# The second SwiGLU's gate and up by seven block products, its down product in three passes

## The chip, the core and the metric

The kernel runs on one core of one Trainium2 chip. The metric is the time of one execution on the device in microseconds (us), the median of several runs. TensorE (PE in the profile) multiplies matrices out of SBUF into PSUM; VectorE (DVE), ScalarE (ACT) and GpSimd (POOL) work on tiles of 128 partitions; SyncE (SP) issues nearly all the loads and stores, in the order of its program.

## What is computed

One layer of a hybrid encoder on 1024 tokens (S) of width 1024 (D): a SwiGLU half-step, a mixer (differential attention beside a bidirectional Mamba-2 scan, one input and one output projection), a second SwiGLU half-step, and a last norm. The width inside a SwiGLU is 2816, which is 22 blocks of 128.

```
def swiglu(x, w_gate, w_up, w_down):
    return (jax.nn.silu(x @ w_gate) * (x @ w_up)) @ w_down

f = swiglu(rmsnorm(h, ffn1_pre_g), ffn1_w_gate, ffn1_w_up, ffn1_w_down)
h = h + 0.5 * rmsnorm(f, ffn1_post_g)
m = hybrid_mixer(rmsnorm(h, mix_pre_g), layer_idx, p)
h = h + rmsnorm(m, mix_post_g)
f = swiglu(rmsnorm(h, ffn2_pre_g), ffn2_w_gate, ffn2_w_up, ffn2_w_down)
h = h + 0.5 * rmsnorm(f, ffn2_post_g)
return rmsnorm(h, final_g)
```

## The kernel before, in words

Every matrix product is done in float32 precision by three matmuls (`mm3`, lines 180 to 182): each operand is split into a high part (a cast on ACT, L174) and a low part (a subtraction, mostly on DVE, L175), and hi·hi, hi·lo and lo·hi are added in PSUM.

The first SwiGLU, up to 717 us, has two halves. `blocks_gate_up` (L304) takes tokens, D and FF in two halves each and needs seven block products for a matrix instead of eight: sums of blocks of the activations stand ready as seven transposed operands b11, b21, b22, t1 to t4 (`blocks_prep`, L259), sums of blocks of the weights are made on the fly on POOL (L363 to L366), and the partial results are joined on DVE. A matrix of 2 FF blocks takes 84 matmuls of 512 columns, a pair of gate and up 168; there are 11 pairs. The product g goes to DRAM (`gd`, L329). `blocks_down` (L418) then goes three times through the 22 FF blocks, for 3, 3 and 2 token tiles, and each pass reads its part of g and all of w_down again; 1056 matmuls in all. What runs around its start is set by pools: the loads of its first weights go into the same ring of three raw buffers that gate and up used.

The mixer follows. Its output projection (`out_rounds`, its additions at L1297 and L1299) runs as filler beside the attention and keeps its sums of all 8 token tiles in SBUF (acc0 to acc7). The last rounds of it are finished at the start of the second SwiGLU.

The second SwiGLU (`ffn`, L462) is direct: for each of 11 chunks of two FF blocks 192 matmuls of gate and up for the 8 token tiles, and 96 of down, whose results are added to acc in SBUF on DVE (L500). g never leaves SBUF. The first and the last chunk work in pieces of 256 columns: `pre2` finishes the output projection tile by tile, adds the residual (`residual`, L237 and L238), norms and transposes (`norm_T`, L208) while the first chunk runs; the last chunk lets each token tile go on to its norms as it is done. Two weight tiles of the first chunk are loaded and split in the end of the attention (`ahead`).

`rstd` (L198 to L200) sums squares on ACT and takes the power on POOL. L165 and L175 are those of one helper for many tiles, so groups are told apart by the tile's name.

In the changed kernel the lines of these functions stand 47 or more lines further down: L165 becomes L212, L175 L222, L208's norm is done at L318, L281 to L284 are L333 to L336, L329 is L381, L434 is L486.

## Time and profile before

| | |
|---|---|
| median of 3 runs | 2638.22 us (2634.17 to 2638.88) |
| the profiled execution | 2636.09 us |
| span in its profile, first to last instruction | 2634.3 us |
| mean granted clock of TensorE | 0.986 |
| first SwiGLU: gate and up / down | about 400 / 250.6 us |
| second SwiGLU, from 1832 us to the end | 802 us |

The profile is of one execution. An engine's busy time counts its instructions; matmuls are pipelined, so that two of them overlap in the listing, and their number in a stretch with its length gives the pitch. In a timeline the bracket behind an instruction is the idle time of its engine before it and what released it. The granted clock is given as a share of full speed.

### The profile page before, as it was taken

Reading aid. Unit: us, or ns where it says so; the run is one execution under the profiler, and the core shown is the slowest. Engines: PE = TensorE matmul, PEld = TensorE weight load, DVE = VectorE, ACT = ScalarE, POOL = GpSimd, SP = SyncE. Lnnn points to the kernel's source line nnn. Section 1 sums busy time; section 2 is a strip of 40 time slices with the busy share of each in tenths; the row PEclk is TensorE's granted clock in tenths of the full one; section 3 lists DMA queues with packets and bytes.
Section 4 is the critical chain, followed back from the end, with each engine's and each line's share of the span. In section 5 each row is a group of like instructions: output and inputs, shape, how many; then the busy total and the mean of one; then the engine's idle time right before and its main releaser. Section 6 shows DMA issues by size and latency. Waiting matters only on the chain.

```text
span 2634.3 us, 32959 instructions
## 1 busy us (share of the span) xinstructions
PE 2524.5 (96%) x12504; PEld 2121.9 (81%) x12504; DVE 1518.2 (58%) x2125; ACT 1003.1 (38%) x1709; POOL 818.9 (31%) x748
## 2 busy tenths in 40 slices
PE   6999999999999999999979999999999999999996
PEld 4888888888888898877758888888888888888885
DVE  7655554464736553777737888888723333333336
ACT  5333222343535543454436555555431111111113
POOL 7332321020210474344326666666300000000005
PEclk8999999999999999999989999999999999999998
DMA  4222222755722675555464444451521111111112
GB/s 152 88 80 74 95 82 78 243 200 174 254 93 94 177 245 199 166 185 182 133 176 106 117 113 123 103 146 53 173 66 35 48 48 48 49 48 48 48 41 104
DMA packets 133406, 309.07 MB, mean 117 GB/s; under 512 B 13696, under 2 KB 62720, under 8 KB 128384
## 3 DMA queue, kind: packets, MB, share of 16 engines
q1 hardware_dynamic: 114912, 245.37, 28.1%
q0 software_dynamic: 10016, 57.42, 8.1%
q10 hardware_dynamic: 8320, 4.19, 0.5%
q8 instruction: 98, 1.61, 0.3%
q14 instruction: 60, 0.49, 0.1%
HBM read 227.50 MB, written 79.43 MB: 117 GB/s over the span
## 4 chain that ended last, share of the span: by engine, by line
PE 83%; DVE 6%; ACT 3%; POOL 3%; issue 2%; DMA 2%; SPq 0%; DVEq 0%; POOLq 0%; ACTq 0%
PE po L182 7%; PE po L180 7%; PE po L181 7%; PE b L180 5%; PE b L181 5%; PE b L182 5%; PE pp L180 5%; PE pp L181 5%; PE pp L182 5%; PE pg L180 3%; PE pg L181 3%; PE pg L182 3%; PE pu L181 3%; PE pu L180 3%; PE pu L182 3%
## 5 line engine op out<-in xcount | busy, mean ns | idle before, releaser
L199 POOL TENSOR_SCALAR rstd<-rstd 128x1 f32<-128x1 f32 x64 | 29.1, 454 | 982.1 <-ACT junk L198 981.1
L175 DVE TENSOR_TENSOR split<-raw,split 128x1024 fp32r<-128x1024 f32 (+3 forms) x220 | 249.9, 1142 | 128.1 <-ACT split L174 127.2
L174 ACT CAST split<-raw 128x1024 fp32r<-128x1024 f32 (+3 forms) x227 | 192.8, 860 | 237.4 <-issue 86.9
L500 DVE TENSOR_TENSOR acc<-acc,po 128x512 f32<-128x512 f32 x160 | 108.6, 686 | 210.4 <-PE po L182 210.3
L1044 ACT ACTIVATE e<-sc,st 128x1024 f32<-128x1024 f32 x128 | 143.3, 1120 | 165.1 <-DVE st L1040 165.1
L180 PE MATMUL pp<-hT,split 128*128 128x512 f32 x384 | 153.4, 399 | 10.5 <-DVE o L909 10.5
L1040 DVE TENSOR_REDUCE st<-sc 128x1 f32<-128x1024 f32 x128 | 150.5, 1217 | 12.6 <-PE sc L1038 12.6
L181 PE MATMUL pp<-hT,split 128*128 128x512 f32 x384 | 151.9, 396 | 0.0
L182 PE MATMUL pp<-hT,split 128*128 128x512 f32 x384 | 151.9, 396 | 0.0
L180 PE MATMUL po<-odd,g 128*128 128x512 f32 x352 | 138.6, 396 | 7.0 <-DVE acc L500 7.0
L181 PE MATMUL po<-odd,g 128*128 128x512 f32 x352 | 138.2, 392 | 0.0
L182 PE MATMUL po<-odd,g 128*128 128x512 f32 x352 | 138.1, 394 | 0.0
L181 PE MATMUL b<-hT,split 128*128 128x512 f32 x352 | 137.8, 391 | 0.3 <-DVE attc L1008 0.3
L182 PE MATMUL b<-hT,split 128*128 128x512 f32 x352 | 137.6, 391 | 0.0
L180 PE MATMUL b<-hT,split 128*128 128x512 f32 x352 | 137.5, 392 | 0.1
L1051 POOL TENSOR_SCALAR e<-e,st 128x768 f32<-128x768 f32 x64 | 75.7, 1182 | 181.7 <-DVE st L1050 138.2
L182 PE MATMUL po<-split,gs 128*128 128x512 f32 x334 | 131.9, 395 | 0.0
L181 PE MATMUL po<-split,gs 128*128 128x512 f32 x334 | 131.9, 395 | 0.0
L180 PE MATMUL po<-split,gs 128*128 128x512 f32 x334 | 131.3, 395 | 0.0
L1053 POOL TENSOR_TENSOR e<-e,e 128x768 f32<-128x768 f32 x64 | 118.3, 1848 | 5.4
L174 ACT CAST g<-sg 128x512 fp32r<-128x512 f32 (+1 forms) x52 | 28.7, 552 | 238.5 <-DVE acc L500 107.8
L180 PE MATMUL pp<-split,hT 128*128 128x512 f32 (+1 forms) x320 | 117.4, 367 | 0.0
(376 smaller groups left out, 7240.7 us busy)
## 6 DMA issues: line engine op xcount, KB each, us to landing
raw<-in_w_down_dram SPq DMA_DIRECT2D x88, 512.0 KB
raw<-in_w_gate_dram SPq DMA_DIRECT2D x45, 512.0 KB
raw<-in_w_up_dram SPq DMA_DIRECT2D x45, 512.0 KB
qkd<-o SPq DMA_DIRECT2D x64, 256.0 KB
qk<-qkd POOLq DMA_DIRECT2D x16, 1024.0 KB, 7.9
gd<-w SPq DMA_DIRECT2D x43, 256.0 KB
vd<-o SPq DMA_DIRECT2D x32, 256.0 KB
kb<-qkd POOLq DMA_DIRECT2D x16, 512.0 KB, 5.2
```

The lines of the kernel that those rows point to most:

```text
L174: self.nc.scalar.copy(out=hi, in_=src)
L175: (eng or self.nc.vector).tensor_tensor(out=lo, in0=src, in1=hi.bitcast(F32), op=ALU.subtract)
L180: mm(out=out, lhsT=a[0], rhs=b[0], start=start, stop=False, **kw)
L181: mm(out=out, lhsT=a[0], rhs=b[1], start=False, stop=False, **kw)
L182: mm(out=out, lhsT=a[1], rhs=b[0], start=False, stop=stop, **kw)
L199: nc.gpsimd.tensor_scalar(out=r[:, 1:2], in0=r[:, 0:1], scalar1=k / n, scalar2=k * EPS, op0=ALU.mult, op1=ALU.add)
L500: nc.vector.tensor_tensor(out=a[:, ns], in0=a[:, ns], in1=po[n], op=ALU.add)
L1040: nc.vector.tensor_reduce(out=X["st"][:, j:j + 1], in_=pc, op=ALU.max, axis=AX.X, negate=True)
L1044: self.nc.scalar.activation(out=X["e", j], in_=X["sc", j], func=AF.Exp, bias=st[:, j:j + 1], accum_out=st[:, 2 + j:3 + j])
L1051: G.tensor_scalar(out=e1[:, XD:], in0=e1[:, XD:], scalar1=st[:, 5:6], scalar2=0.0, op0=ALU.mult, op1=ALU.add)
L1053: G.tensor_tensor(out=e0[:, XD:], in0=e0[:, XD:], in1=e1[:, XD:], op=ALU.add)
```

## The change

The second SwiGLU is written like the first. `blocks_prep` is run for all 8 token tiles on acc itself, with the sums of a tile pair written over acc[t-4]; `blocks_gate_up` is called with a new ring, LateRing, whose buffers are those that the output projection and the attention leave: one raw tile of its own and one that was `wo`'s, acc5 to acc7 later; two split tiles of its own and two halves of the attention's `qk` tile; acc0 to acc4 in halves for partial results. t2 and t3 lie in `wo`, t4 in the attention's `kb` and `v`. `early` finishes the output projection, prepares the tiles, and runs the first products of pairs 0 and 1 between them. Nothing is loaded ahead in the attention's end (`iter(())`). When gate and up are done all these pools are closed, new ones are opened (`ring3`, `gp2`, `fp2`, norms, gains), and `blocks_down` runs with g from DRAM (`gd2`) and the two gains loaded when token tile 0 is done.

The diff, without its blank lines:

```diff
@@ -120,6 +120,53 @@
             return self.halves(tag, lambda: first)
         k = self.turn[tag] = (self.turn.get(tag, -1) + 1) % n
         return self.whole(first + k)
+class LateRing:
+    def __init__(self, rp, wo, hp, mp, accp):
+        self.rp, self.wo, self.hp, self.mp, self.accp = rp, wo, hp, mp, accp
+        self.raws = [lambda: rp.tile([P, D], F32, tag="raw", name="raw", bufs=1), lambda: wo.tile([P, D], F32, tag="raw", name="raw", bufs=1)]
+        self.splits = [self.own, self.own]
+        self.half, self.next, self.rest = None, 0, None
+    def own(self):
+        return self.rp.tile([P, 2, D], F32R, tag="split", name="split", bufs=2)
+    def pair(self):
+        if self.rest is None:
+            t = self.hp.tile([P, 4, D], F32R, tag="qk", name="qk", bufs=1)
+            self.rest = t[:, 2:4, :]
+            return t[:, 0:2, :]
+        t, self.rest = self.rest, None
+        return t
+    def place(self, i):
+        return self.accp.tile([P, D], F32, tag=f"acc{i}", name=f"acc{i}", bufs=1)
+    def grow(self):
+        self.raws += [lambda i=i: self.place(i) for i in (5, 6, 7)]
+        self.splits += [self.pair, self.pair]
+    def load(self, cols):
+        return Ring.turn(self.raws)()
+    def take(self, cols):
+        return Ring.turn(self.splits)()
+    def tile(self, shape, dtype, tag, name, bufs):
+        if tag == "s":
+            return self.hp.tile([P, 512], F32R, tag="half", name="s", bufs=3).bitcast(F32)
+        if tag == "u":
+            return self.mp.tile([P, 2, 2, P], F32R, tag="mhl", name="u", bufs=3).rearrange("p s k l -> p (s k l)").bitcast(F32)
+        if self.half is None:
+            self.half = self.place(self.next % 5)
+            self.next += 1
+            return self.half[:, 0:512]
+        h, self.half = self.half, None
+        return h[:, 512:1024]
 class Banks:
@@ -256,6 +303,11 @@
             self.move()
+    @staticmethod
+    def blocks(h0, h1):
+        return {n: (h[:, 0, d:d + 4, :], h[:, 1, d:d + 4, :]) for n, h, d in (("b11", h0, 0), ("b21", h0, 4), ("b22", h1, 0), ("t1", h1, 4))}
     def blocks_prep(self, tags, x, y, ps, gain, C, t, junk=None):
@@ -270,7 +322,7 @@
             pt = ps.tile([P, 4, P], F32, "b", "pt", 8)
             for i in range(4):
                 nc.tensor.transpose(out=pt[:, i, :], in_=s[:, i * P:(i + 1) * P], identity=self.ident)
-            self.split(pt, C[n][:, 0, :, ts], C[n][:, 1, :, ts])
+            self.split(pt, C[n][0][:, :, ts], C[n][1][:, :, ts])
         x0, x1 = x[:, 0:512], x[:, 512:1024]
         if t < 4:
@@ -323,7 +375,7 @@
             for d in range(4):
                 ds = slice(d * P, (d + 1) * P)
-                self.mm3(p, (u[0][:, ds], u[1][:, ds]), (C[n][:, 0, d, :], C[n][:, 1, d, :]), d == 0 and not more, d == 3, skip_group_check=more)
+                self.mm3(p, (u[0][:, ds], u[1][:, ds]), (C[n][0][:, d, :], C[n][1][:, d, :]), d == 0 and not more, d == 3, skip_group_check=more)
         def store(sg, f, h):
             nc.sync.dma_start(out=gd[f][:, h * 512:(h + 1) * 512], in_=sg)
@@ -1338,8 +1390,10 @@
             with ExitStack() as cb:
                 xp = k.pool(cb, "blocks")
                 h0, h1b = k.new_halves()
-                C = dict(b11=h0[:, :, 0:4, :], b21=h0[:, :, 4:8, :], b22=h1b[:, :, 0:4, :], t1=h1b[:, :, 4:8, :])
-                C.update({n: xp.tile([P, 2, 4, 512], F32R, name=n) for n in ("t2", "t3", "t4")})
+                C = k.blocks(h0, h1b)
+                for n in ("t2", "t3", "t4"):
+                    t = xp.tile([P, 2, 4, 512], F32R, name=n)
+                    C[n] = (t[:, 0], t[:, 1])
                 spool = k.pool(cb, "sums")
                 tags = Tags(k.pool(cb, "work"), 5)
@@ -1457,15 +1511,13 @@
         hctx.close()
         hctx = ExitStack()
-        acc = k.acc = k.new_acc(k.pool(hctx, "acco", side="left"))
+        accp = k.pool(hctx, "acco", side="left")
+        acc = k.acc = k.new_acc(accp)
         k.mp = k.pool(hctx, "mp", side="left")
         ps = k.pool(c5, "ps4", space=PSUM)
         ps.tile([P, 4, P], F32, tag="pt", name="pt", bufs=2)
         ap = k.pool(c5, "ap", side="left")
-        ring2 = HeadRing(wo, hp)
-        gus, g2 = [], {}
-        gu = k.gate_up_units(ring2, a["w_gate2"], a["w_up2"], 0)
-        ahead = (gus.append(next(gu)) for _ in range(2))
+        g2 = {}
         def prepare():
             g2["rows"] = rows = HeadRows(hp)
@@ -1474,37 +1526,53 @@
             k.early[1] = k.load_rows(rows, h1, 1)
             g2["pre"] = k.gain(rows, a["ffn2_pre_g"])
-        k.attention(hp, ap, ps, H, fill, ahead, prepare)
+        k.attention(hp, ap, ps, H, fill, iter(()), prepare)
         nrm = g2["rows"]
         c5.close()
         with c4:
-            k.hpool = k.pool(hctx, "hT2", side="left")
-            rp = ring2.rest = k.pool(hctx, "ring2", side="left")
-            ringd = Ring(rp, 1, wo, 2, "odd")
-            ps = k.pool(c4, "ps5", space=PSUM)
-            k.bank = lambda: ps.tile([P, 512], F32, tag="pgu", name="pgu", bufs=4)
-            nrm.rows["x"].insert(0, rp.tile([P, D], F32, name="x"))
-            halves = k.new_halves()
-            gus += gu
-            def pre2(t0):
-                for t in range(t0 + 2 if t0 else 0, min(t0 + 4, T)):
-                    k.move()
+            hp2 = k.pool(hctx, "hT2", side="left")
+            rp = k.pool(hctx, "ring2", side="left")
+            ring2 = LateRing(rp, wo, hp, k.mp, accp)
+            nrm.rows["t2"] = [rp.tile([P, 512], F32, name="t2")]
+            ps = Banks(k.pool(c4, "ps5", space=PSUM))
+            k.hpool = hp2
+            C = k.blocks(*k.new_halves())
+            def early(begun, held):
+                ps.turn = [0, 1, 2, 3]
+                k.bank = lambda: ps.tile([P, 512], F32, "b", "po", 8)
+                for t in range(T):
                     while t not in k.mixed:
                         next(fill)
-                    steps = k.residual(nrm, acc[t], t, h1, g2["mix"], 1.0, h2, nc.gpsimd if t < 6 else nc.vector,
-                                       lambda f, x, t: k.norm_T(nrm, ps, f, x, t, g2["pre"], halves))
-                    next(steps)
-                    k.running.append(steps)
-                if t0 == 0:
-                    for _ in range(9):
-                        next(fill)
+                    if t == T - 1:
+                        for _ in fill:
+                            pass
+                        for n, pool, tags in (("t2", wo, ("odd", "odd")), ("t3", wo, ("even", "even")), ("t4", hp, ("kb", "v"))):
+                            C[n] = [pool.tile([P, 4, 512], F32R, tag=x, name=n, bufs=1 if pool is hp else 2) for x in tags]
+                        gate, up = begun(0, (4, 5))
+                        gate()
+                    k.push(k.residual(nrm, acc[t], t, h1, g2["mix"], 1.0, h2, nc.gpsimd if t < 4 else nc.vector,
+                                      lambda f, x, t: k.blocks_prep(nrm, f, acc[t - 4], ps, g2["pre"], C, t)))
+                up()
                 k.move()
-                if t0 == T - 2:
-                    k.finish()
-                    g2["post"] = k.gain(nrm, a["ffn2_post_g"])
-                    g2["final"] = k.gain(nrm, a["final_g"])
+                gate, up = held(1, (6, 7))
+                gate()
+                k.move()
+                up()
+                k.finish()
+                ring2.grow()
+            gd2 = dr([NF, P, S], F32, name="gd2")
+            k.blocks_gate_up(ring2, ring2, ring2, ps, C, a["w_gate2"], a["w_up2"], gd2, early)
+        hctx.close()
+        with ExitStack() as c6:
+            ps = Banks(k.pool(c6, "ps6", space=PSUM))
+            rp = k.pool(c6, "ring3")
+            ring = Ring(rp, 3, rp, 6)
+            nrm, gains = norm_pools(c6)
+            gp, fp = k.pool(c6, "gp2"), k.pool(c6, "fp2")
+            g2 = {}
             def final(f, x, t):
                 r = k.rstd(nrm, f)
@@ -1515,13 +1583,13 @@
                     nc.vector.scalar_tensor_tensor(out=f[:, cs], in0=f[:, cs], scalar=r, in1=g2["final"][:, cs], op0=ALU.mult, op1=ALU.mult)
                     nc.sync.dma_start(out=out[t * P:(t + 1) * P, cs], in_=f[:, cs])
-            def post3(t, acc):
-                k.push(k.residual(nrm, acc, t, h2, g2["post"], 0.5, None, nc.gpsimd if t < 6 else nc.vector, final))
-            k.ffn(ring2, ringd, lambda: wo.tile([P, 2, 1024], F32R, tag="even", name="g", bufs=2),
-                  lambda: hp.tile([P, 512], F32R, tag="half", name="sg", bufs=3).bitcast(F32), ps, acc, halves, a["w_gate2"], a["w_up2"], a["w_down2"], pre2, post3, gus)
-            k.finish()
-        hctx.close()
+            def post3(t, f):
+                if t == 0:
+                    g2["post"] = k.gain(gains, a["ffn2_post_g"])
+                    g2["final"] = k.gain(gains, a["final_g"])
+                k.push(k.residual(nrm, f, t, h2, g2["post"], 0.5, None, nc.gpsimd if t < 6 else nc.vector, final))
+            k.blocks_down(ring, gp, fp, ps, gd2, a["w_down2"], post3, iter(()))
 def layout(inputs):
```

How the instructions stand now. PE before, in the middle of the second SwiGLU: pg is the gate's bank, po the down product's, hT the normed tokens, g the activations.

```order
L180 MATMUL pg<-hT_15489,split 128x512
L181 MATMUL pg<-hT_15489,split 128x512
L180 MATMUL po<-odd,g 128x512
L181 MATMUL po<-odd,g 128x512
L182 MATMUL po<-odd,g 128x512
```

PE in the changed kernel, where its gate and up end; b is a product's bank, t_15768 is t4, po the first bank of down.

```order
L229 MATMUL b<-t_15768,split 128x512
L227 MATMUL b<-t_15768,split 128x512
L228 MATMUL b<-t_15769,split 128x512
L229 MATMUL b<-t_15768,split 128x512
L227 MATMUL po<-split 128x512 x6
L228 MATMUL po<-split 128x512
L229 MATMUL po<-split 128x512
```

Gate, up and down were in turns in each chunk; now all of down stands behind all of gate and up.

SP at such a seam: first as it stands at the first SwiGLU's in both kernels, with the semaphores that each row waits for (DMAHW and DMASW are DMA queues).

```order
L165 DMA raw<-gd 128x384 [waits DMAHW6_49,DVE_49]
L165 DMA raw<-in_w_down_dram 128x1024 [waits DMAHW7_49,DVE_49]
L165 DMA raw<-gd 128x384 [waits DMAHW4_49,DVE_49]
L165 DMA raw<-in_w_down_dram 128x1024 [waits DMAHW5_49,DMAHW0_49,DVE_49]
L165 DMA raw<-in_w_down_dram 128x1024 [waits DMAHW6_49,DMAHW1_49,DVE_49]
L329 DMA gd<-w_3012 128x512 [waits DMAHW2_49,DVE_49]
L329 DMA gd<-w_3095 128x512 [waits DMAHW3_49,DVE_49]
```

And SP at the second SwiGLU's seam in the changed kernel; acc are the halves in which g is made, x the rows of h2 for the residual.

```order
L381 DMA gd_15481<-acc_18638 128x512 [waits DMAHW7_49,DVE_49]
L212 DMA raw<-gd_15481 128x384 [waits DMASW3_49,DMAHW0_49,DMASW2_49,PE_49]
L212 DMA raw<-in_w_down_dram 128x1024 [waits DMAHW1_49,DMASW4_49]
L212 DMA raw<-gd_15481 128x384 [waits DMAHW2_49]
L486 DMA graw<-gd_15481 128x384 [waits DMAHW3_49,Activation_49,Pool_49]
L381 DMA gd_15481<-acc_18556 128x512 [waits DMAHW4_49,DVE_49]
L486 DMA graw<-gd_15481 128x384 [waits DMAHW5_49]
L486 DMA graw<-gd_15481 128x384 [waits DMAHW6_49]
L212 DMA raw<-in_w_down_dram 128x1024 [waits DMAHW7_49,DMAHW0_49,DVE_49]
L234 DMA gain<-in_ffn_post_g_dram 128x1024
L234 DMA gain<-in_final_g_dram 128x1024 [waits DMAHW1_49]
L275 DMA x<-h_70 128x1024 [waits DMAHW2_49]
```

At the first seam the loads for down stand among the stores of g and wait for DVE alone. At the second the first of them waits for PE, and the semaphore's value is that of the last product with t4, since the new ring lies over `kb` and `v`; the others stand behind it, with the gains and x between the second and the third load of w_down.

POOL while the tiles are prepared, before (residual additions and the small rstd operations):

```order
L199 TENSOR_SCALAR rstd<-rstd 128x1
L200 TENSOR_TENSOR rstd<-rstd,mhalf 128x1
L238 TENSOR_TENSOR acc_10545<-qk,acc_10545 128x1024
L199 TENSOR_SCALAR rstd<-rstd 128x1
L200 TENSOR_TENSOR rstd<-rstd,mhalf 128x1
```

And POOL there in the changed kernel:

```order
L333 TENSOR_TENSOR acc_10542<-acc_10546,acc_10542 128x512
L335 TENSOR_TENSOR acc_10546<-acc_10546 128x512
L222 TENSOR_TENSOR split<-raw,split 128x512 x2
L336 TENSOR_TENSOR acc_10542<-acc_10542,t_15475 128x512
L246 TENSOR_SCALAR rstd<-rstd 128x1
L247 TENSOR_TENSOR rstd<-rstd,mhalf 128x1
L246 TENSOR_SCALAR rstd<-rstd 128x1
L247 TENSOR_TENSOR rstd<-rstd,mhalf 128x1
L415 TENSOR_TENSOR s<-raw 128x512
```

POOL has the sums of the blocks, splits of weights and sums of weights there besides.

## Rows read from the trace of the kernel before

**Rows 1.** The page: busy time of each engine, and the chain that ended last

```profile
PE 2524.5 (96%) x12504; PEld 2121.9 (81%) x12504; DVE 1518.2 (58%) x2125; ACT 1003.1 (38%) x1709; POOL 818.9 (31%) x748
...
PE 83%; DVE 6%; ACT 3%; POOL 3%; issue 2%; DMA 2%; SPq 0%; DVEq 0%; POOLq 0%; ACTq 0%
```

**Rows 2.** Windows: length, PE, PEld, DVE, ACT, POOL busy, clock, DMA, GB/s

```profile
126.97:431.61 304.64, 304.64 (x1345) 252.25 (x1344) 173.73 (x224) 90.88 (x160) 96.02 (x64) 1.00 0.24 82
466.50:717.10 250.60, 250.60 (x1106) 204.06 (x1106) 148.75 (x165) 117.27 (x176) 33.68 (x30) 1.00 0.66 220
475.00:485.00 10.00, 10.00 (x45) 8.19 (x44) 2.65 (x3) 3.21 (x4) 0.00 (x0) 1.00 0.91 353
1831.85:1900.00 68.15, 61.67 (x385) 54.45 (x385) 53.26 (x69) 32.73 (x59) 30.86 (x36) 0.95 0.43 148
1850.50:1855.50 5.00, 5.00 (x17) 4.21 (x16) 5.00 (x7) 2.51 (x6) 2.02 (x3) 0.50 0.30 124
2014.88:2412.96 398.08, 398.08 (x1730) 324.70 (x1729) 139.71 (x180) 64.50 (x85) 0.00 (x0) 1.00 0.15 48
2617.20:2634.30 17.10, 0.41 (x2) 0.00 (x0) 10.56 (x11) 4.01 (x8) 7.86 (x10) 0.59 0.32 123
```

**Rows 3.** ACT's timeline: start, duration, instruction, idle before it and releaser

```profile
126.97 0.59 ACT L375 COPY w<-b 128x512 f32<-128x512 f32 x1 [1.53 <-PE b L182]
...
2014.88 0.60 ACT L481 ACTIVATE sg<-pg 128x512 f32<-128x512 f32 x1 [1.05 <-PE pg L182]
```

**Rows 4.** DVE's timeline where the two kernels part, at 1831 us

```profile
1830.65 1.28 DVE L237 SCALAR_TENSOR_TENSOR acc<-acc,rstd,qk 128x1024 f32<-128x1024 f32 x1
1831.85 0.68 DVE L1297 TENSOR_TENSOR acc<-acc,sc 128x512 f32<-128x512 f32 x1
```

**Rows 5.** DVE's groups by shape, 1831.85 to 1900 us: busy, mean, idle

```profile
L237 DVE SCALAR_TENSOR_TENSOR acc<-acc,rstd,qk 128x1024 f32<-128x1024 f32 x7 | 9.0, 1279 | 1.5 <-POOL rstd L200 1.5
L208 DVE SCALAR_TENSOR_TENSOR qk<-acc,rstd,qk 128x1024 f32<-128x1024 f32 x5 | 8.5, 1700 | 3.0 <-POOL rstd L200 3.0
L175 DVE TENSOR_TENSOR hT<-pt,hT 128x512 fp32r<-128x512 f32 x12 | 7.9, 682 | 5.2 <-ACT hT L174 5.2
L1299 DVE SCALAR_TENSOR_TENSOR acc<-pgu,vv,acc 128x512 f32<-128x512 f32 x11 | 7.7, 738 | 0.0
...
L175 DVE TENSOR_TENSOR mhl<-mraw,mhl 128x256 fp32r<-128x256 f32 x3 | 4.8, 1596 | 0.0
```

**Rows 6.** DVE's groups by shape in the first SwiGLU's preparation, 20 to 66 us

```profile
L266 DVE SCALAR_TENSOR_TENSOR w<-w,rstd,w 128x1024 f32<-128x1024 f32 x4 | 8.2, 2044 | 2.5 <-POOL rstd L200 2.5
...
L175 DVE TENSOR_TENSOR split<-raw,split 128x512 fp32r<-128x512 f32 x4 | 5.5, 1400 | 0.0
L282 DVE TENSOR_TENSOR w<-w,split 128x512 f32<-128x512 f32 x4 | 4.9, 1230 | 0.0
```

**Rows 7.** POOL's groups, 20 to 66 us

```profile
L284 POOL TENSOR_TENSOR split<-split,w 128x512 f32<-128x512 f32 x4 | 6.1, 1528 | 0.6 <-ACT split L174 0.6
```

**Rows 8.** POOL's groups, 1831.85 to 1900 us

```profile
L200 POOL TENSOR_TENSOR rstd<-rstd,mhalf 128x1 f32<-128x1 f32 x13 | 8.3, 636 | 1.1
```

**Rows 9.** Timeline of POOL and DVE, 1845.7 to 1846 us

```profile
1845.73 2.36 POOL L175 TENSOR_TENSOR split<-raw,split 128x1024 fp32r<-128x1024 f32 x1
1845.80 3.37 DVE L208 SCALAR_TENSOR_TENSOR qk<-acc,rstd,qk 128x1024 f32<-128x1024 f32 x1 [2.31 <-POOL rstd L200]
```

**Rows 10.** SP's timeline, the loads ahead of the first SwiGLU's down product

```profile
419.75 0.33 SPq L165 DMA_DIRECT2D raw<-gd  x1
...
462.72 0.33 SPq L165 DMA_DIRECT2D raw<-in_w_down_dram  x1
```

**Rows 11.** A weight load of 512 KB on SP's timeline

```profile
1937.38 0.33 SPq L165 DMA_DIRECT2D raw<-in_w_up_dram  x1
```

**Rows 12.** The cast on ACT that waits for that load

```profile
1940.54 1.05 ACT L174 CAST split<-raw 128x1024 fp32r<-128x1024 f32 x1 [4.45 <-DMA raw<-in_w_up_dram]
```

**Rows 13.** PE's timeline after a stall, at 1850 us

```profile
1849.89 0.79 PE L180 MATMUL pgu<-odd,mhl 128*128 128x512 f32 x1 [3.38 <-DVE acc L1299]
```

## The prediction

> **What bounds the kernel now.** I read the page first. TensorE is busy 96% of the span and makes 83% of the chain that ended last [rows 1], so matmuls taken away are time taken away wherever PE runs without a pause. The windows say where: over six regular chunks of the second SwiGLU PE is busy for all of the 398.08 us at full clock, while DVE works a third of it, POOL not at all and the DMA carries 48 GB/s [rows 2]. The window's edges are one SiLU and the same SiLU six chunks later; the first edge stands in [rows 3]. Six chunks hold 6 x 288 = 1728 matmuls, so one costs 398.08/1728 = 0.2304 us, and a chunk 66.35.
>
> The stretch where the first SwiGLU does what the second is now to do comes next. From the first copy of a pair's bank [rows 3] to the one eight pairs later are 304.64 us, PE busy in all of them at full clock [rows 2]: 38.08 for a pair of 168 matmuls, 0.2267 each. Nothing else is near its limit there: DVE 57%, ACT 30%, POOL 32%, DMA 24%. The down product behind it runs 250.60 us without a pause [rows 2]; of these 1056 x 0.2267 = 239.4 are its matmuls, and the rest is the normed tokens' transposes.
>
> Then DVE, because the changed kernel puts more on it at one place. From 1831.85 to 1900 us it is busy 53.26 of 68.15 us, POOL 30.86 [rows 2].
>
> **The change part by part.** Up to DVE's addition at 1831.85 [rows 4] the two kernels do the same, but for the two weight tiles that are no longer loaded in the attention's end; I cost that at nothing, since PE is then at the attention's matmuls (minus 3 to plus 1: at most the two splits that leave). So the sum is counted from 1831.85.
>
> *Preparation, from there to the last low part of t3 on DVE*, behind which PE's products run freely. PE has in it 90 matmuls of the output projection, 108 of the first products (72 begun and held, 36 after) and 112 transposes: (90 + 108) x 0.2267 + 112 x 0.13 (estimate: a transpose's quarter of the columns, with something for its start) = 60 us. DVE has more:
> - 12 additions at 0.68 [rows 4] and 12 at 0.74 [rows 5]: 17.0
> - 27 low parts from PSUM at 0.68 [rows 5]: 18.4
> - 7 residual multiplications and 8 norms, 1024 columns with two operands in SBUF, at 1.28 [rows 5]: 19.2
> - 4 residual additions of 1024 columns (t of 4 and above now on DVE; before only 6 and 7) at 1.22, which I take from the 1.23 of [rows 6]: 4.9
> - 4 block differences and 8 low parts of weight halves, 512 columns: 0.68 each if they go like PSUM's, 8.2
> - 3 low parts of mixed tiles at 1.60 [rows 5], 4.8, and 1.9 of small ones.
>
> Together 74.4. One starts 0.08 before the last one's listed end (1830.65 + 1.28 against 1831.85 [rows 4]), which over 91 takes 7 off: 67 is the floor. But two-operand work stretches beside POOL. A norm took 1.70 on average [rows 5] and 2.04 in the first SwiGLU's preparation, where the weights' low parts took 1.40 and the block differences 1.23 [rows 6]. The second preparation gives POOL the same work: 12 block operations, 6 weight splits, 9 weight sums, 4 additions, 16 pairs of rstd, by the rows 27 x 1.5 [rows 7], 4 x 2.4 (as the split of [rows 9]) and 16 x 1.0 = 66 us (0.64 for a pair's second operation [rows 8], an estimated 0.4 for its first). So I price by [rows 6]: 8 norms + 8 x 0.76, 8 low parts + 8 x 0.72, 4 differences + 4 x 0.55 = 14.1, and half of 8.2 for the residual operations, if these stretch as the norms do: 67 + 14 + 4 = 85. Idle time of DVE was 22% before, where it did not set the pace; with the pace its own I take 8 us. That gives 93, so PE runs free at 1925. Bounds: 72 (the floor, 5 idle) and 107 (below).
>
> *Gate and up.* 11 x 168 = 1848, less the 108 done: 1740 x 0.2267 = 394.4 [rows 2], +2 because the second SwiGLU's pitch was 0.2304 until now (by that 400.9; bounds 394 to 401). End 2321.4. The partial sums, SiLU, weight sums and stores of g are hidden under PE as in the first SwiGLU, by the engines' shares above. LateRing has 4 split tiles where the first had 6, so 8 halves; a product uses one for 12 x 0.2267 = 2.7 us, which leaves 21 us of reach, against 3.2 us for a load of 512 KB [rows 11, 12] and about 3 for cast and low part.
>
> *The seam.* In the first SwiGLU the loads for down were issued from 419.75 to 462.72, up to 47 us ahead of the end of gate and up at 466.5, where the window of down begins [rows 2, 10], and PE did not stop. Now SP's first load waits for the last product with t4, because its buffer lies over `kb` and `v`. Behind that wait on SP stand the loads of g and of w_down, a last store of g, the gains and x; ACT, DVE and at last PE wait for them. From the last product: 0.5 for release and issue, 3.2 for 512 KB [rows 11, 12], 1.05 for the cast [rows 12], 1.2 for the low part: first matmul of down after about 6. The second w_down is there in time for it (2.0 MB queued at 353 GB/s, [rows 2], 5.6 us; needed 4.1 after the first). The third stands behind gains and x: 4.7 MB / 353 = 13.4 + 0.9 + 2.3 = 16.6 against 14 needed: 2.7 more. After a stall of 3.38 us [rows 13] PE ran at a granted clock of 0.50 for the next 5 us [rows 2], the lower of its two levels (1.2 GHz of 2.4), and so lost 2.5 of them, with the edges 2.8. Sum 11.5; bounds 6 (first wait alone) and 25 (4.7 MB at 200 GB/s, and the clock).
>
> *Down.* 239.4 + 2.6 for its waits at bank changes = 242, without the first one's transposes. DMA has room: 704 KB for 18 matmuls, 4.1 us, is 173 GB/s. End 2574.9. The 160 additions of down's partial results on DVE go; they were hidden but for some waits in the last chunk, which I cost at nothing.
>
> *Tail.* Before, 17.10 us from the last matmul to the end [rows 2], DVE busy for 10.56. Now both last tiles end within 1.4 us, so that DVE has one tile's residual and norm more in the chain (3.8 us), but not the last chunk's left-over work. I take 17.1 (bounds 15 and 21).
>
> Sum: 1831.85 + 93 + 396.4 + 11.5 + 242 + 17.1 = 2591.9 us of span, 42.4 below 2634.3. The profiled execution took 2636.09, 1.8 over its span, and the median is 2.1 above that: 2595.8, so 2595. Checked another way: a regular chunk 66.35 becomes 38.08 + 242/11 = 60.08, and nine of them save 56; the ends of the SwiGLU give 14 back.
>
> **The rivals.** *Less stretch, short seam.* If DVE keeps its floor, 72, and the seam costs 6: 2595.8 - 21 - 5.5 = 2569. For it: the 1.28 of the residual operations beside a POOL that was working [rows 5]. Against it: [rows 6].
>
> *DVE and POOL take turns.* A norm that began 0.07 us after a POOL split of 2.36 us took 3.37 instead of 1.28 [rows 9]: it waited the split out and then ran. If all work of two SBUF operands on DVE goes so against all of POOL's, the preparation is 19.2 + 4.9 + 8.2 + 1.7 (mixed) = 34, plus POOL's 66, plus 7 idle: 107; and with a seam at 20 the time is 2595.8 + 14 + 8.5 = 2618. Against it: much of POOL's rstd work waits for ACT and falls beside PSUM work on DVE, and in [rows 5] seven residual operations of the same shape kept to 1.28.
>
> The Trainium skill has this as a rule (SBUF — State Buffer, section "SBUF: two separate sides"): a DVE operation with two SBUF inputs and a GpSimd operation that reads SBUF share a port pair as an exclusive lock, and the loser blocks for the whole instruction. The pair of rows agrees, and the rule speaks against this change; by it the time is this rival's 2618.
>
> *Starved gate and up: slower.* With 8 halves and raw tiles freed late, PE could wait in every pair. 42.4 us are gained, and 1740/168 = 10.4 pairs remain, so it decides from 38.08 + 42.4/10.4 = 42.2 us for a pair; at 44 the time is 2595.8 + 5.9 x 10.4 = 2657. For it: half of the split tiles are parts of `qk`, available late, and POOL's sums need three s tiles. Against it: 21 us of reach, and POOL at 32%.
>
> *No change.* Preparation at 120 and seam at 25 together give 2595.8 + 27 + 13.5 = 2636. That the seven products don't save what they say is excluded by the count: gate and up were 1728 matmuls of 512 columns and 768 of 256, worth 2112, and are 1848.
>
> **How the numbers follow.** Forecast 2595: 55% (its own range 2580 to 2607). Less stretch: 15%. Taking turns: 20%. Starved: 5%. No change: 5%. The range from 2570 to 2620 reaches to both neighbours and leaves out the last two and some of the edges. A measurement of this kernel tells about 0.2%, 5.3 us, from no change; the first three cases are faster by more: 0.90, with 0.05 on each of the others.
>
> **What would show it.** In the changed kernel's profile: DVE over 85% busy from 1832 to some 1925, its norms near 2 us; pairs 38.1 to 38.7 us apart in the SiLU rows; PE idle some 6 us once at the seam and some 3 a little later, its wait ending with ACT or DVE behind a DMA; a down of about 242. The forecast is wrong if pairs take over 40 us, if PE waits for POOL or the DMA inside gate and up, or if the preparation ends before 1905 or after 1940.

## The result, and the profile after

The changed kernel takes 2607.22 us (median of 4 runs, 2606.38 to 2608.16) against 2638.55 of the kernel before: a ratio of 0.9884 with a 95% interval of 0.9867 to 0.9901, 31 us or 1.2% less. Forecast were 2595 and a range of 2570 to 2620, so the forecast was right in its direction, and 12 us too low; the measured time is at the upper edge of the forecast's own range, 2580 to 2607.

The new profile's span is 2604.6 us; the sum had 2591.9. The windows of the changed kernel, cut where the prediction's terms end (length; PE, PEld, DVE, ACT and POOL busy; granted clock; DMA share; GB/s):

```profile
1831.85:1925.46 93.61, 70.19 (x309) 54.91 (x308) 79.81 (x89) 44.07 (x80) 66.57 (x62) 0.82 0.40 134
1925.46:2331.75 406.29, 406.29 (x1761) 329.95 (x1760) 218.56 (x292) 113.96 (x202) 117.15 (x79) 1.00 0.23 75
2331.75:2588.06 256.31, 248.56 (x1057) 200.28 (x1056) 143.97 (x153) 111.54 (x164) 34.40 (x30) 0.99 0.65 216
2588.06:2604.60 16.54, 0.39 (x2) 0.00 (x0) 8.23 (x8) 4.82 (x9) 4.57 (x8) 0.62 0.16 63
1985.50:2296.19 310.69, 310.69 (x1345) 252.28 (x1344) 168.11 (x224) 90.12 (x161) 95.02 (x64) 1.00 0.24 78
```

The edges are the end of DVE's last low part of t3 (1925.46), the start of the last product's last matmul (2331.75) and that of down's last (2588.06). Beside the prediction:

| term | predicted | measured |
|---|---|---|
| preparation, from 1831.85 | 93 | 93.6 |
| gate and up behind it | 396.4 | 406.3 |
| seam and down | 11.5 + 242 | 256.3 |
| tail | 17.1 | 16.5 |

Of the 12.7 us that the sum missed, 9.9 are in gate and up and 2.8 in the seam and down. The last window answers to the first SwiGLU's row of [rows 2]: eight pairs of 168 matmuls each, PE busy without a pause, clock 1.00, in both; 304.64 us there and 310.69 here. Its edges are these copies on ACT, as in [rows 3]:

```profile
1985.50 0.59 ACT L427 COPY acc<-b 128x512 f32<-128x512 f32 x1 [7.16 <-PE b L229]
...
2296.19 0.59 ACT L427 COPY acc<-b 128x512 f32<-128x512 f32 x1 [7.16 <-PE b L229]
```

So a matmul of the same form costs 0.2312 us instead of 0.2267, with no wait of PE to blame.

DVE's groups in the changed kernel's preparation, 1831.85 to 1925.46 us (busy, mean ns, idle before):

```profile
L318 DVE SCALAR_TENSOR_TENSOR acc<-acc,rstd,qk 128x1024 f32<-128x1024 f32 x8 | 14.2, 1773 | 0.1
L284 DVE SCALAR_TENSOR_TENSOR acc<-acc,rstd,qk 128x1024 f32<-128x1024 f32 x7 | 11.4, 1635 | 0.0
...
L285 DVE TENSOR_TENSOR acc<-qk,acc 128x1024 f32<-128x1024 f32 x4 | 6.9, 1714 | 0.0
...
L334 DVE TENSOR_TENSOR t<-acc,acc 128x512 f32<-128x512 f32 x4 | 5.4, 1340 | 0.0
```

The norms take 1.77 instead of 1.28 us, the residual multiplications 1.64, the additions 1.71: the stretch beside POOL that was priced with [rows 5, 6] is there. The waits of PE from 1831 us on:

```profile
PE pt L324 <- DVE hT L222: 7.8, 3, 4.5
PE po L227 <- ACT split L221: 7.5, 2, 5.5
PE pt L324 <- POOL acc L333: 4.5, 1, 4.5
```

The second line is the seam. On PE's timeline these are its two stalls, with down's first matmuls behind them:

```profile
2337.69 0.79 PE L227 MATMUL po<-split 128*128 128x512 f32 x1 [5.54 <-ACT split L221]
...
2350.51 0.50 PE L227 MATMUL po<-split 128*128 128x512 f32 x1 [1.96 <-ACT split L221]
```

and on SP's the first loads for down, 0.4 us after the last product began its last matmul, where [rows 10] had them up to 47 us ahead:

```profile
2332.18 0.32 SPq L212 DMA_DIRECT2D raw<-gd  x1
2332.59 0.38 SPq L212 DMA_DIRECT2D raw<-in_w_down_dram  x1
```

One more row of the same profile suggested what to test. In the first SwiGLU's down product the first three blocks take g from the split ring, all later ones from tiles gs of another pool; nothing else differs. PE's groups from 466 to 480 us, and then from 480 to 700:

```profile
L227 PE MATMUL po<-split 128*128 128x512 f32 x18 | 7.0, 389 | 0.0
```

```profile
L228 PE MATMUL po<-split,gs 128*128 128x512 f32 x308 | 121.7, 395 | 0.0
```

389 ns against 395 each (the listed duration holds what overlaps with the next one; the difference is that of the pitch). The tiles' addresses in the compiled program say how they lie: gs begins 96 bytes past a multiple of 256 in its partition, the splits 224. In the first gate and up all operands are at 224. In the second hT and two split tiles are at 32, qk and t4 at 96, t2 and t3 at 224.

### The profile page after: what moved, and what is told of

Read it like the earlier page. It is cut to its first block, busy times and chain, and to the rows that moved or that the text cites. A ratio compares the mean times of both kernels' runs of the same rounds, so it can differ in the third digit from the quotient of the medians.

```text
span 2604.6 us, 32787 instructions
## 1 busy us (share of the span) xinstructions
PE 2480.4 (95%) x11904; PEld 2065.6 (79%) x11904; DVE 1646.9 (63%) x2258; ACT 1103.3 (42%) x1895; POOL 969.7 (37%) x849
## 4 chain that ended last, share of the span: by engine, by line
PE 81%; DVE 6%; POOL 4%; ACT 3%; DMA 3%; issue 3%; SPq 0%; DVEq 0%; POOLq 0%; ACTq 0%
PE b L227 11%; PE b L228 11%; PE b L229 11%; PE po L229 7%; PE po L227 7%; PE po L228 7%; PE pp L227 5%; PE pp L228 5%; PE pp L229 5%; PE pgu L229 2%; PE pgu L227 2%; PE sc L1090 2%; PE sc L1089 2%; PE pgu L228 2%; PE pt L1113 1%
## 5 line engine op out<-in xcount | busy, mean ns | idle before, releaser
L222 DVE TENSOR_TENSOR split<-raw,split 128x1024 fp32r<-128x1024 f32 (+3 forms) x284 | 328.1, 1161 | 144.3 <-ACT split L221 139.9
L221 ACT CAST split<-raw 128x1024 fp32r<-128x1024 f32 (+3 forms) x296 | 253.7, 867 | 259.1 <-issue 86.9
L228 PE MATMUL po<-split,gs 128*128 128x512 f32 x668 | 263.7, 395 | 0.0
L229 PE MATMUL po<-split,gs 128*128 128x512 f32 x668 | 263.4, 395 | 0.2 <-DVE gs L222 0.2
L227 PE MATMUL po<-split,gs 128*128 128x512 f32 x668 | 260.9, 395 | 0.0
L227 PE MATMUL b<-hT,split 128*128 128x512 f32 x548 | 214.7, 393 | 0.0
L229 PE MATMUL b<-hT,split 128*128 128x512 f32 x548 | 214.4, 391 | 0.0
L228 PE MATMUL b<-hT,split 128*128 128x512 f32 x548 | 214.2, 391 | 0.0
L227 PE MATMUL b<-t,split 128*128 128x512 f32 x396 | 155.3, 392 | 0.1
L228 PE MATMUL b<-t,split 128*128 128x512 f32 x396 | 155.2, 392 | 0.0
L229 PE MATMUL b<-t,split 128*128 128x512 f32 x396 | 154.6, 391 | 0.0
L229 PEld LDWEIGHTS po<-split,gs 128*128 128x128 f32 x668 | 125.8, 188 | 30.2 <-DVE gs L222 1.0
L227 PEld LDWEIGHTS po<-split,gs 128*128 128x128 f32 x668 | 125.8, 188 | 29.4 <-ACT split L221 0.2
L415 POOL TENSOR_TENSOR s<-raw 128x512 f32<-128x512 f32 x31 | 43.2, 1393 | 284.4 <-DMA raw<-in_w_up_dram 128.8
L228 PEld LDWEIGHTS po<-split,gs 128*128 128x128 f32 x668 | 125.8, 188 | 29.0
L222 DVE TENSOR_TENSOR gs<-graw,gs 128x384 fp32r<-128x384 f32 (+1 forms) x126 | 73.7, 586 | 114.8 <-ACT gs L221 114.7
```

The source lines that it names most:

```text
L221: self.nc.scalar.copy(out=hi, in_=src)
L222: (eng or self.nc.vector).tensor_tensor(out=lo, in0=src, in1=hi.bitcast(F32), op=ALU.subtract)
L227: mm(out=out, lhsT=a[0], rhs=b[0], start=start, stop=False, **kw)
L228: mm(out=out, lhsT=a[0], rhs=b[1], start=False, stop=False, **kw)
L229: mm(out=out, lhsT=a[1], rhs=b[0], start=False, stop=stop, **kw)
L415: G.tensor_tensor(out=s1, in0=a21, in1=a22, op=ALU.add)
```

## The experiments

The theory after this reading: a matmul's pitch depends on whether its two operands lie at the same place modulo 256 bytes (called *place* below). Its rival (*company*): the pitch is the stage's, set by what the other engines and the DMA do beside PE. The prediction's two other terms, the seam and the stretch of DVE, are tested by taking each away.

**e1: hT and the own splits to 224.**

```diff
+            k.pool(hctx, "pad", side="left").tile([P, 48], F32, name="pad")
             hp2 = k.pool(hctx, "hT2", side="left")
```

> A pad of 192 bytes in each partition ahead of hT2 and ring2; nothing else. Theory (place): a matmul of 512 columns costs 0.2267 us where its moving and its stationary operand lie at the same place modulo 256 bytes in their partition, and 0.232 to 0.2335 where not. In the changed kernel hT and the own split tiles lie at 32, qk and t4 at 96, t2 and t3 at 224; after the pad hT and the own splits are at 224. Then the own splits match in six products of seven, and qk only in t4's: a mean of 0.2297 instead of 0.2312, a pair in 38.6 us instead of 38.84, about 2.5 us off the whole gate and up. Rival (company): the pitch is that of the stage, by what ACT, DVE, POOL and the DMA do beside PE; then a pair stays at 38.84 and the time at the changed kernel's 0.988 of the kernel before.

Measured 2608.69 us, ratio 0.9893 (0.9878 to 0.9908): no gain that the time can show. In its profile eight pairs take 309.45 us (from a product's last matmul to the same one eight pairs on), 1.2 less than 310.69 where 2.0 were expected. The direction fits place, the size is 60% of what it gave. With splits of both kinds the offset changes every few products, and after a change the pitch needed some eight matmuls to settle: products at the same place took 0.2275 us a matmul with the own splits and 0.2293 with qk (from the starts of successive matmuls in the trace), not 0.2267.

**e2: all operands of the second gate and up to 224.** With e1's pad:

```diff
+            hp.tile([P, 32], F32, name="pad2")
             nrm.rows["t2"] = [rp.tile([P, 512], F32, name="t2")]
```

> The pad of e1 and 128 bytes more at the end of the attention's pool hp, which move qk, kb, v (t4) from 96 to 224: all operands of the second gate and up at the same place modulo 256. Place: a pair falls to 38.08 us as in the first SwiGLU, 8 pairs to 304.7 us from 310.69, the whole kernel to about 2599 us (8 us less than the changed kernel). Company: 38.84 a pair and no change in the time.

Measured 2601.01 us, ratio 0.9864 (0.9848 to 0.9881): 6.2 under the changed kernel, where 8 were expected. The copies on ACT that begin and end eight pairs in e2's profile:

```profile
2005.03 0.59 ACT L427 COPY acc<-b 128x512 f32<-128x512 f32 x1 [1.14 <-PE b L229]
...
2309.67 0.59 ACT L427 COPY acc<-b 128x512 f32<-128x512 f32 x1 [1.14 <-PE b L229]
```

304.64 us, to the hundredth the first SwiGLU's [rows 2]. The instructions and their neighbours are those of the changed kernel; only 320 bytes of padding are new. For gate and up, company has fallen.

**e5: g of both down products to the splits' place.**

```diff
             k.blocks_down(ring, gp, fp, ps, k.gd, a["w_down1"], post1, z)
+            gp.tile([P, 32], F32, name="gpad")
...
             k.blocks_down(ring, gp, fp, ps, gd2, a["w_down2"], post3, iter(()))
+            gp.tile([P, 32], F32, name="gpad2")
```

> 128 bytes at the end of the pools gp and gp2, which move the tiles gs (g, the stationary operand of both down products) from 96 to 224, where the w_down splits lie; gate and up untouched. Place: po<-split,gs goes from 0.2324 to 0.2267 a matmul, each down product loses 6 us (the first from 250.6 to about 244.6), the kernel 12, to about 2595 us. Company: both down products stay.

Measured 2597.95 us, ratio 0.9855 (0.984 to 0.9869). The two down products in the changed kernel, from their first matmul to their last, and in e5:

```profile
467.73:717.87 250.14, 250.14 (x1104) 203.66 (x1103) 147.71 (x165) 117.22 (x176) 33.92 (x30) 1.00 0.67 220
2337.69:2588.06 250.37, 248.16 (x1055) 200.28 (x1056) 142.02 (x150) 109.98 (x162) 34.40 (x30) 0.99 0.65 215
```

```profile
467.42:712.74 245.32, 245.07 (x1105) 202.84 (x1104) 147.79 (x165) 117.44 (x176) 33.98 (x30) 1.00 0.67 224
2333.71:2578.91 245.20, 242.54 (x1056) 199.49 (x1056) 141.78 (x150) 109.75 (x162) 34.29 (x30) 0.99 0.65 220
```

5 us from each, where 6 were expected; the time falls by 9, where 12 were. The first SwiGLU's down, which the change doesn't touch, gains like the second's.

**e3: the seam without the late wait.** No pool is closed between up and down; a class lays down's tiles over those that come free:

```diff
-        hctx.close()
-        with ExitStack() as c6:
-            ps = Banks(k.pool(c6, "ps6", space=PSUM))
-            rp = k.pool(c6, "ring3")
-            ring = Ring(rp, 3, rp, 6)
-            nrm, gains = norm_pools(c6)
-            gp, fp = k.pool(c6, "gp2"), k.pool(c6, "fp2")
+            ring = nrm = gains = gp = fp = LateDown(ring2, wo, hp, hp2, accp)
...
+        flat = [hpool.tile([P, 2, 8, 512], F32R, tag=f"hT{i}", name=f"hT{i}", bufs=1).rearrange("p s d t -> p (s d t)") for i in range(2)]
...
+        more = [cut(flat[0], i * 2048, 2048).rearrange("p (s c) -> p s c", s=2) for i in range(4)]
+        ring.splits = [lambda m=m: m for m in more] + [ring.own, ring.own]
+        at = 32
+        rows = [wo.tile([P, 2, D], F32R, tag=x, name="rows", bufs=2).bitcast(F32) for x in ("odd", "odd", "even")]
+        rows = [r[:, i, :] for r in rows for i in range(2)]
+        self.rows = {"gs": [cut(flat[1], at + i * 768, 768).rearrange("p (s c) -> p s c", s=2) for i in range(4)],
+                     "graw": [cut(flat[1], at + 3072 + i * 384, 384).bitcast(F32) for i in range(3)],
+                     "x": rows[0:3], "gain": rows[3:5]}
```

> The seam: the pools of the second gate and up stay open through down; raw tiles, splits (over hT0), g (over hT1), x and gains are laid over tiles by name, so that SP's first loads for down wait for raw tiles that come free some 15 us ahead and not for the last product with t4. The g tiles stay 128 bytes off the splits, so the pitch of down is as before. Theory (the first load's wait makes the seam): PE's 5.54 us wait between the last product and down's first matmul and the 1.96 us one behind it go, with the half clock after them, 9 to 10 us in all, to about 2598 us. Rival (the load is only the first of several): the casts on ACT, the low parts on DVE behind the last g's multiplication, or the gains in the DMA, end later than the last product, PE waits 3 to 5 us for DVE there and the time falls by no more than 4.

Measured 2597.76 us, ratio 0.9853 (0.9838 to 0.9868): 9.5 less than the changed kernel. SP's first loads for down in e3's profile, and PE at the seam:

```profile
2305.29 0.32 SPq L245 DMA_DIRECT2D raw<-gd  x1
2311.46 0.33 SPq L245 DMA_DIRECT2D acc<-in_w_down_dram  x1
```

```profile
2336.68 0.39 PE L262 MATMUL b<-t,split 128*128 128x512 f32 x1
2336.91 1.32 PE L260 MATMUL po<-hT 128*128 128x512 f32 x5
```

The loads go out 31 us ahead, and down begins 0.23 us after the last product, one pitch. No wait for ACT is left in PE's list there, and down itself, at the same offset of 128 bytes, takes 244.91 us from first to last matmul instead of 250.37. So the seam was 5.7 us before down's first matmul (2337.69 - 2331.75 less one pitch) and 5.5 behind it: 11.2. The time fell by less, 9.5; what lies between is ahead of these stages (see the table after e8).

**e4: POOL's tile work of the second preparation on DVE.**

```diff
-        V, G = nc.vector, nc.gpsimd
+        V, G = nc.vector, nc.vector if self.late else nc.gpsimd
...
-                product(p, unit(r[:, 0:512], G), "b11")
+                product(p, unit(r[:, 0:512], V if self.late else G), "b11")
...
-  ... g2["mix"], 1.0, h2, nc.gpsimd if t < 4 else nc.vector,
+  ... g2["mix"], 1.0, h2, nc.vector,
```

> In the second preparation all of POOL's work on whole tiles goes to DVE: the 12 block sums, the 6 low parts of the begun and held products' weights, the 4 residual additions of tiles 0 to 3. POOL keeps rstd and the weight sums. Theory (turns): DVE's operations with two operands in SBUF were stretched by POOL (8 norms 1.77 us, 7 residual multiplications 1.64, 4 additions 1.71, 4 differences 1.34, instead of 1.28, 1.28, 1.22, 0.68, together some 14 us); without POOL's work they fall to 1.2 to 1.4, DVE has 15 us more of its own work at undisturbed durations and 11 to 13 less of stretch, and the preparation ends within 4 us of the changed kernel's: about 2608 to 2611 us. Rival (no turns): the stretch comes from PE's or the DMA's traffic; the durations stay, the preparation ends 15 us later and the time is about 2622 us.

Measured 2601.76 us, ratio 0.987 (0.9855 to 0.9885): 5.5 under the changed kernel by the medians. The two ratios' intervals overlap, so it is the stage's length that carries the reading. Both expectations missed, turns by some 8 us and no turns by 20. The mechanism is the first one's, as DVE's groups in e4 show (1831.85 to 1920 us):

```profile
L285 DVE TENSOR_TENSOR acc<-qk,acc 128x1024 f32<-128x1024 f32 x8 | 10.1, 1265 | 0.0
L284 DVE SCALAR_TENSOR_TENSOR acc<-acc,rstd,qk 128x1024 f32<-128x1024 f32 x7 | 9.0, 1280 | 0.1
...
L336 DVE TENSOR_TENSOR t<-acc,acc 128x512 f32<-128x512 f32 x4 | 2.7, 685 | 0.3 <-PE pt L326 0.3
L335 DVE TENSOR_TENSOR acc<-acc,acc 128x512 f32<-128x512 f32 x4 | 2.7, 683 | 0.0
```

Without this work on POOL 1.64 is 1.28, 1.71 is 1.27, 1.34 is 0.685, and the block sums that took POOL 1.28 to 1.51 us take DVE 0.68. The 8 norms fall less far, from 1.77 to 1.40; POOL still makes its weight sums then. Measured from the attention's last matmul, which ends some us earlier or later from profile to profile (1824 to 1836), the preparation ended after 84.3 us in e4 and after 92.8 to 94.5 in six kernels with the sums on POOL. DVE's busy time came out near the 2 to 4 us more that were expected: 81.5 us by 1917.47 us, the preparation's end in e4, instead of 79.8. What the expectation left out is DVE's idle time, 4.1 of 85.6 us instead of 13.8 of 93.6. Its cause may be the handing over between engines (in the changed kernel PE waits 4.5 us for one sum on POOL); that wasn't tested by itself. The whole time gains less than the stage, since PE had by then done 80 matmuls of the products and not 92: 12 more at 0.2314 are 2.8 us.

**e7: the kernel before, with the pads alone** (192 bytes ahead of hT2, 128 in hp, 128 in gp, as in e1, e2 and e5).

> The kernel before, with the pads alone: 192 bytes ahead of hT2, 128 at the end of hp, 128 in gp. Place: its second SwiGLU's matmuls go from 0.2304 to 0.2267 us, 3168 of them (in units of 512 columns) 11.7 us, and the first down product loses 6: about 2620 us. Company: no change, 2638.

Measured 2620.9 us, ratio 0.9945 (0.9929 to 0.9962). Five regular chunks of its second SwiGLU take 326.40 us (one SiLU at 2006.79, the same at 2333.19): 65.28 a chunk instead of 66.35, or 0.2267 a matmul.

**e6: e2, e3 and e5 together.**

> e2, e3 and e5 together: all operands of the second gate and up, and of both down products, at the same place modulo 256 bytes, and the seam with open pools. If the three gains are of separate places they add: 8 (gate and up) + 10 (seam) + 12 (both down products) = 30 us under the changed kernel's 2607, about 2578 us. Rival: PE's faster matmuls meet the next limit (loads of down at 4.1 us a block in the first pass, or casts on ACT) and the seam or down gives 5 us or more back: 2583 or later.

Measured 2576.68 us, ratio 0.9772 (0.9757 to 0.9786), 30.5 under the changed kernel. The eight pairs and the second down product, with no offset, in e6's windows:

```profile
2014.48:2319.11 304.63, 304.63 (x1345) 252.25 (x1344) 164.55 (x222) 89.97 (x159) 82.88 (x56) 1.00 0.27 89
2319.34:2558.50 239.16, 239.16 (x1056) 197.97 (x1055) 139.09 (x150) 107.58 (x159) 33.58 (x30) 1.00 0.63 211
```

**e8: e6 with e4.**

> e6 with e4: same places modulo 256 in the second SwiGLU and in both down products, pools kept open over the seam, and POOL's tile work of the preparation on DVE. If the gains are of separate places, e4's 5 us come off e6's 2576.7: about 2572 us. Rival: e6's and e4's gains share the stretch of low clock around the end of the preparation, and less than 2 us comes off: 2575 or more.

Measured 2570.37 us, ratio 0.9753 (0.9739 to 0.9766): 6.3 under e6, and the best of all, 37 us under the changed kernel. The intervals of e6 and e8 overlap a little.

A firmer comparison leaves out what varies from profile to profile ahead of the second SwiGLU. From the end of the attention's last matmul to the end of the span the profiles have:

| changed kernel | e1 | e2 | e5 | e3 | e4 | e6 | e8 |
|---|---|---|---|---|---|---|---|
| 773.2 | 772.4 | 765.1 | 767.6 | 762.4 | 766.9 | 747.2 | 740.5 |

So e2 gains 8.1 us, e3 10.8, e4 6.3, and e8 6.7 on e6. In e5 and e6 the first down product's 5 us come on top, since it lies ahead of the attention.

**e9: the offset by itself.** In e8 the place of gs against the splits is one number (`at`, in words of 4 bytes); three kernels set it to 16, 48 and 64.

```diff
-        at = 0
+        at = 16
```

> e8 with the second down product's tiles gs moved by 64 bytes against the w_down splits. Place modulo 256: its 1056 matmuls take more than 239.2 us, the length that they took in e6 with no offset; by the rows of the changed kernel's t1 and t4 products at 64 some 0.229 to 0.231 each, 242 to 244 us. Rival (only a half of the 256 counts, or the offset matters modulo 64): 239.2.

> e8 with gs moved by 192 bytes. Place modulo 256: slow, by the rows of the changed kernel's products at 192 some 0.233 each, 246 us. Rival (modulo 64 or 192 harmless): 239.2 us.

> e8 with gs moved by 256 bytes. Place modulo 256: as without an offset, 239.2 us. Rival (any shift of gs costs, or the bank at a larger period): 242 us or more.

The second down product from its first to its last matmul, in e8 itself and then at 64, 192 and 256 bytes:

```profile
2309.01:2548.17 239.16, 239.16 (x1057) 197.98 (x1055) 138.93 (x150) 107.78 (x159) 33.63 (x30) 1.00 0.63 210
```

```profile
2314.54:2560.35 245.81, 245.81 (x1057) 198.32 (x1055) 138.99 (x150) 107.45 (x159) 32.85 (x30) 1.00 0.62 205
```

```profile
2313.11:2554.47 241.36, 241.36 (x1057) 198.12 (x1055) 139.12 (x150) 107.76 (x159) 33.72 (x30) 1.00 0.63 208
```

```profile
2310.33:2549.48 239.15, 239.15 (x1056) 197.98 (x1055) 139.14 (x150) 107.77 (x159) 33.73 (x30) 1.00 0.63 210
```

Their times, one execution each, are 2578.55, 2572.7 and 2567.81 us. PE never pauses in any of these windows. The figure at 128 is e3's (another kernel, whose splits lie at 32 and gs at 160):

| offset, bytes | 0 | 64 | 128 | 192 | 256 |
|---|---|---|---|---|---|
| down, us | 239.16 | 245.81 | 244.91 | 241.36 | 239.15 |
| us per matmul (of 1055 steps) | 0.2267 | 0.2330 | 0.2321 | 0.2288 | 0.2267 |

Zero and 256 agree to a hundredth. The first three blocks (54 of the 1056 matmuls) have their g in the split ring, which doesn't move; the others alone took 0.2333 at 64, 0.2324 at 128 and 0.2289 at 192. The loaded g behind gs moves along with it.

64 was expected milder and 192 worse than they came out, because the expectations seem to have taken the offset the other way round. Counted as in the table, from the moving operand up to the stationary one, the changed kernel's own products agree with it: hT with qk and t3 or t2 with the own splits, at 64, took 0.2330, and t4 with the own splits, at 192, took 0.2302. So the order of the two operands counts, and an offset of 64 costs more than one of 192.

## Why the prediction was right, and what it missed

*Preparation: right in size (93 predicted, 93.6 measured), near in its parts.* DVE did not set the pace as closely as priced: 79.8 us busy and 13.8 idle instead of 85 and 8, with norms at 1.77 instead of the 2.04 of [rows 6]. Two misses of 5 to 6 us cancelled, so that the closeness of the sum is luck. That it set the pace at all, and lost time to POOL, e4 shows. One assumption beside it failed: PE was to have 108 of the products' matmuls done by then and had 92; 16 matmuls are 3.7 us of the next term. The output projection had 99 left in the stretch, not 90, and after its stalls PE ran at a granted clock of 0.66 from 1917.5 to 1925.5 us, which cost 2.7 us, or 12 matmuls.

*Gate and up: the step that failed.* "1740 x 0.2267 = 394.4 [rows 2], +2 because the second SwiGLU's pitch was 0.2304 until now". 1756 matmuls were left and took 0.2314 each, 406.3 us, which is outside the term's bounds of 394 to 401; a pair took 38.84 us, over the 38.1 to 38.7 that the prediction gave as its sign. The two pitches stood side by side in [rows 2], and the forecast took the pitch of a stage of the same form and not that of the buffers. The change moves the work into the second SwiGLU's buffers, and the pitch is theirs: e2 and e7 give 0.2267 to both ways of computing it by padding alone. Weighed as a cause of its own it would have given 1756 x (0.2314 - 0.2267) = 8.2 us more than counted, less the 2 allowed, which with the 3.7 above is the term's miss of 9.9.

*Seam: right.* Predicted 11.5, and 11.2 by e3; the stalls were 5.54 us (6 predicted) and 1.96 (2.7), both ending with ACT's cast behind a DMA. After the first of them PE ran at a granted clock of 0.51 for 5.2 us, which costs 2.6 (2.8 predicted); after the second the clock was 1.00. About 1 us of the 11.2 is in none of these. The wait is the one named: e3 takes it away and PE goes on without a step.

*Down: 242 predicted, 245 measured without the seam's share*, again the place: at 128 bytes of offset 244.9, at none 239.2. The 2.6 us that the prediction allowed for waits at bank changes are in no run (PE never paused in e6's 239.16), and 5.7 for the offset were missing, so the nearness of 242 is luck. The first SwiGLU's 250.1, from which the 242 came, was not matmuls at 0.2267 with transposes in the rest, as the prediction had it, but matmuls at 0.232 for the most part (e5: 245.3 without the offset).

*Tail: right*, 16.5 for 17.1.

*The rivals.* Less stretch, short seam: no, the stretch was there. Turns: that POOL's tile work stretches DVE's operations is shown in e4; whether an operation waits out a whole one of the other engine isn't told apart there. The Trainium skill's rule (SBUF — State Buffer, "SBUF: two separate sides": an exclusive lock on the pair of ports) agrees with durations that fall to 1.28 and 0.68 once that work is gone. The rival's price, 107 us for the preparation, was not reached: DVE and POOL were busy for 79.8 and 66.6 us of 93.6, so for at least 52.8 us both at once. Starved gate and up: no, PE had no pause in 310.69 us and four split tiles are enough. No change: no.

Still open is why an offset between the operands costs what it does, and why 64 and 192 bytes differ; the runs show the cost, not its reason. Whether the place of the result in PSUM has a part wasn't tried, nor were offsets that are no multiple of 64.

## What to carry to other kernels

A pitch read in one stage belongs to its buffers as well as to its instructions: before moving work into other buffers, compare the pitch of matmuls that already use these, and see how the operands lie modulo 256 bytes; a few small tiles at the head of a pool are enough to shift all that lie behind them. Where a stage follows another in new pools, the first load's wait is for the last reader of whatever lay at that address, so lay the first tiles over buffers that come free early. Work given to GpSimd to relieve VectorE can cost both: here moving it to VectorE gained 8 to 9 us of preparation and about 6 of time.

## What the runs showed of the hardware

- A stream of weight loads and matmuls of 128x128 by 512 columns (fp32r) ran at 0.2267 us a matmul at full clock where moving and stationary operand lay at the same place modulo 256 bytes in the partition, and at 0.2333, 0.2324 and 0.2289 where gs, the stationary one, was 64, 128 or 192 bytes further (e9, and e3 for 128). At 0, 64, 192 and 256 the table above is one product in one kernel, with nothing else changed but the place of the loaded g.
- After a change of the offset from product to product the pitch took some eight matmuls to come back to 0.2267 (e1 and the changed kernel's own products); a mixture of places gains less than its share of good ones.
- A VectorE operation of two SBUF operands took 1.28 us (1024 columns) or 0.68 (512) without GpSimd's tile work beside it, and 1.64 to 1.77 or 1.34 on average with it (e4 and the changed kernel). The norms, also of 1024 columns, took 1.40 in e4, where GpSimd's weight sums stayed.
- The same 12 block sums of 512 columns took 0.68 us each on VectorE and 1.28 to 1.51 on GpSimd.
